# Feature-major projections of a two-layer decoder: one 512-column matmul over the tokens' high and low parts, a second of 256 columns, and four PSUM banks a chunk

## The chip, the cores and the metric

The kernel runs on one core of a Trainium2 chip. Its times are device microseconds: the median of three runs, and one profiled execution from which all rows below come. In the rows PE is the matrix engine (TensorE) and PEld its loading of weights, DVE the vector engine (VectorE), ACT the scalar engine (ScalarE), POOL GpSimd, SP the engine that issues most transfers. PSUM is the memory in which matmuls add up their results; the kernel uses it in banks of 128 x 512 fp32 numbers.

## The reference

256 tokens of width 2048 pass through two layers, each x = x + mixer(rms_norm(x)), and one last norm. The first mixer is a gated linear recurrence (HGRN2), the second a sparse attention with a compressed, a selected and a windowed branch. Both begin with one wide projection and end with an output projection; everything is fp32.

```python
def hgrn2_mixer(h, w_in, lb, head_gain, w_out):
    proj = (h @ w_in).reshape(B, S, 4, HGRN_HEADS, HGRN_HEAD_DIM)
    q, f_pre, v, z = proj[:, :, 0], proj[:, :, 1], proj[:, :, 2], proj[:, :, 3]
    ...
    o = rms_norm(o, head_gain) * jax.nn.silu(z)
    return o.reshape(B, S, HGRN_WIDTH) @ w_out

def nsa_mixer(h, w_in, ...):
    proj = h @ w_in
    q, k_c, v_c, k_s, v_s, k_w, v_w, gate_logits, z = jnp.split(proj, split_at, axis=-1)
    ...
    o = jnp.einsum('bshc,bshcd->bshd', gates, out).reshape(B, S, NSA_WIDTH) * jax.nn.silu(z)
    return o @ w_out
```

## The kernel before, in words

**Precision by parts.** Each fp32 operand of a large product is split into a high part (rounded, of type `fp32r`) and a low part, the rest (`fp32r` as well). A product of a and b is then three matmuls added up in PSUM: high a with high b, high a with low b, low a with high b. `mm3` (L148 to L150) issues them; so nearly all matmuls of the kernel have line L150. The tokens stand transposed in `xh` and `xl`, 16 tiles of 128 features by 256 tokens each.

**Pieces.** All weight matrices are walked in one list, `plan`. An entry is a piece: 128 rows by 1024 columns of weights, loaded by one 512 KB transfer on SP's queue into one of 6 `raw` buffers. For a chunk of 512 output features a piece holds two of the 16 k-tiles. ScalarE casts a piece to its high part (`emit_hi`, L132) and VectorE subtracts to get the low part (`emit_lo`, L142), both some four pieces ahead of TensorE (`SPLIT_AHEAD`), into buffers that come free when TensorE has done with an older piece. So ScalarE's casts and VectorE's subtractions run at TensorE's pace, and while they wait they hold up what is queued behind them.

**Chunks.** A chunk of kind "t" is feature-major: the weights are loaded as the stationary operand, 128 x 128 at a time, and the 256 tokens move past, so that one output tile is 128 features by 256 tokens. There are 20 such chunks of four tiles each: f and hq of four groups in the first layer (forget gate and query), then kc, vc, ks, kw, and q0 to q3 and z0 to z3 in the second. Two tiles share a PSUM bank; a chunk takes two of the pool's four banks (`main_bank`, names `mainps`) and the next chunk the other two. In a piece the k-tile is the outer loop and the tile f the inner one (`feature_major`, L170). 20 chunks x 16 k-tiles x 4 tiles make 1280 groups of three matmuls. A chunk of kind "n" is token-major: the tokens are stationary and 512 columns of weights move.

**What sets the order.** Nothing is reordered afterwards: each engine runs its instructions as the program issues them. `flush` (L249) walks the plan: first what the last chunk left to do (`finished`, the chunk's `done`), then one step of every running generator (`advance`), then the casts and loads that have come due (`prefetch`), then the piece's matmuls, then one more step of every generator. The work after a chunk (scaling by the row norms, the recurrence, the attention of a head) is written as generators whose `yield`s space it over the pieces. So a chunk's results are read from PSUM one iteration after its last matmul, behind that iteration's work. A second pool of four banks (`auxps`) holds scores, logits and transposes.

**The second layer's attention.** For each head, logits go through a biased copy with a maximum on VectorE (L868), exponentials on ScalarE (L875), a division by the sum (L884 and L886), and seven transposes on TensorE (L895 to L898). Buffers named `zs` (two of 128 x 512) hold a chunk's scaled result: kz, ks, qs or zs by turns; for z chunks they end with `yl` (L992), the low part of the gated output.

Of the kernel before, what the change touches and what calls it, by code (L numbers as in the profile page):

```python
# [45 lines left out]
def kernel(ctx: ExitStack, tc: tile.TileContext, x, norm_gains, final_gain, rel_bias,  # L46
# [56 lines left out]
    def add_chunk(w, c0, ncols, kind, src, done=None, before=None, late=False, extra=None, cuts=None):  # L103
        n = max(1, PIECE // ncols)
        if cuts is None:
            cuts = [list(range(k, min(k + n, KT))) for k in range(0, KT, n)]
        ch = dict(w=w, c0=c0, n=ncols, kind=kind, src=src, done=done, before=before, late=late)
        for i, kts in enumerate(cuts):
            plan.append((ch, kts, i == len(cuts) - 1))
            for more in (extra or {}).get(i, ()):  # L110
                more()
# [40 lines left out]
    def emit_products(i, between=None):  # L152
# [6 lines left out]
        if kts[0] == 0:  # L159
            if ch["kind"] == "t":  # L160
                ch["ps"] = [main_bank() for _ in range(n // 256)]
# [8 lines left out]
        def feature_major(k, hv, lv):  # L170
            for f in range(n // P):
                fs = slice(f * P, (f + 1) * P)
                mm3(ch["ps"][f // 2][:, (f % 2) * S:(f % 2 + 1) * S], hv[:, fs], lv[:, fs],
                    ah[:, k, :], al[:, k, :], k == 0 and f % 2 == 0, k == KT - 1)
# [8 lines left out]
        if ch["late"] and kts[0] * n >= PIECE:  # L183
# [6 lines left out]
            return  # L190
        for j, k in enumerate(kts):
            if ch["kind"] == "t":
                feature_major(k, hv[:, j], lv[:, j])
            else:
                token_major(k, hv[:, j], lv[:, j], (0, 1))
            if j == 0 and between:
                between()
# [51 lines left out]
    def flush():  # L249
        start_piece(2)  # L250
        finished = None
        for i, (ch, kts, last) in enumerate(plan):
# [10 lines left out]
            emit_products(i, (lambda: start_piece(i + 3)) if starting else None)  # L263
            if last and ch["done"]:
# [8 lines left out]
    xh = xgp.tile([P, KT, S], F32R, name="xh")  # L273
    xl = xgp.tile([P, KT, S], F32R, name="xl")
# [16 lines left out]
    hgain = pcol[:, 0, 48:49]  # L291

# [116 lines left out]
    def f_of(s, ps):  # L409
        for a in range(2):  # L410
            HG["F", a] = HG["pool"].tile([P, 512], F32, tag=f"Fg{a}", name="Fg")
            HG["K", a] = HG["pool"].tile([P, 512], F32, tag=f"Kg{a}", name="Kg")
            nc.vector.tensor_mul(pair(HG["K", a]), pair(ps[a]), rb2)
# [18 lines left out]
    def q_done(ps):  # L432
        for a in range(2):
            QQ = HG["pool"].tile([P, 2, 512], F32, tag=f"QQ{a}", name="QQ")
            nc.vector.tensor_mul(pair(QQ[:, 0]), pair(ps[a]), rbq2)
            HG["Q", a] = QQ

# [132 lines left out]
    for s in range(4):  # L570
        def on_f(ps, s=s):
            if s == 0:
                open_hg()
            if s == 0:
                run(bcast_rows(rbc, rbcq, rstd0))
                run(store_bias(), 8)
            run(f_of(s, ps), 1 if s == 0 else 0)

        def on_q(ps):
            q_done(ps)  # L580
# [8 lines left out]
        add_chunk(w_in1, 2048 + 512 * s, 512, "t", X, on_f, before=split_x if s == 0 else None,  # L589
                  cuts=[[0], [1]] + [[k, k + 1] for k in range(2, KT, 2)] if s == 0 else None)  # L590
        add_chunk(w_in1, 512 * s, 512, "t", X, on_q)
# [96 lines left out]

    def kc_done(name, *args):
        def done(ps):  # L690
            if name == "kc":
                open_ns()
            kz = [NS["p2"].tile([P, 2, S], F32, tag="zs", name="kz") for _ in range(2)]
            for j in range(2):
                nc.vector.tensor_mul(kz[j], pair(ps[j]), rb2)
# [59 lines left out]
    def split_of(src, hi, lo, col=None):  # L755
# [6 lines left out]
        yield  # L762
        yield
# [21 lines left out]
    def k_done(off):  # L785
        def done(ps):
            ks = [NS["p2"].tile([P, 2, S], F32, tag="zs", name="ks") for _ in range(2)]
            for j in range(2):
                nc.vector.tensor_mul(ks[j], pair(ps[j]), rb2)
# [7 lines left out]
    def vw_done(j):  # L797
        n = 280 if j == 0 else 232

        def done(ps):  # L800
            gate = NS["gate"]
            run(split_of([p[:, :n] for p in ps], *([t[:, tt, 280 * j:280 * j + n] for tt in range(2)] for t in NS["Vw"]),
                         [rstd1[:, tt:tt + 1] for tt in range(2)]))
# [10 lines left out]
    def q_done1(g):  # L814
        def done(ps):
            qs = [NS["p2"].tile([P, 2, S], F32, tag="zs", name="qs") for _ in range(2)]
            for a in range(2):
                nc.vector.tensor_mul(qs[a], pair(ps[a]), rbq2)
# [144 lines left out]
    def z_done1(g):  # L963
        def done(ps):
            run(gated(g, ps, NS.pop(("o", g))))
        return done

    def gated(g, ps, ov):
        ks = [slice(4 * g + 2 * a, 4 * g + 2 * a + 2) for a in range(2)]
        zs = [NS["p2"].tile([P, 2, S], F32, tag="zs", name="zs") for _ in range(2)]  # L970
# [170 lines left out]
```

## Time and profile before

| | |
|---|---|
| median of 3 runs | 993.58 us (993.15 to 994.56) |
| profiled execution | 993.57 us |
| its span (first to last instruction) | 991.7 us |
| mean granted TensorE clock, of 1 | 0.998 |
| TensorE busy | 978.8 us |
| VectorE, ScalarE busy | 630.3 us, 519.1 us |
| moved by DMA | 179.14 MB |

The profiled execution takes 1.9 us more than its span. Busy times of TensorE overlap, since a matmul is issued while the one before it is still running: a matmul's row gives its start and its duration from issue to end, and the time that it costs TensorE is the distance to the next start. In rows of a timeline the first number is the start in us from the span's start, the second the time that the engine was busy with the row's instructions (x2 are two of a kind in a row), then engine, line, operation, the tile that is written and the tiles that are read, and their shapes. In square brackets stands the idle time ahead of it, and what ended it.

### The profile page before, as it was taken

To read this page: it belongs to the slowest core of one execution; us is meant where nothing else is said; L and a number is where in the kernel's file an instruction comes from. 1 tells how busy PE (TensorE), PEld (TensorE's weight loads), DVE (VectorE), ACT (ScalarE), POOL (GpSimd) and SP (SyncE) were. 2 spreads that over 40 slices of the span, in tenths; PEclk is the share of its full clock that TensorE was granted. 3 is DMA by queue.
4 is the path that set the end of the run, shared out by engine and by line. 5 is a ranking of instruction groups with operands and counts; after the bars stand their busy time and mean duration, and the time that the engine had idled before them with its cause. 6 is when DMAs were issued, how large, how long until landed. Compare 5 with 4: busy or idle time off the path is not lost.

```text
span 991.7 us, 19895 instructions
## 1 busy us (share of the span) xinstructions
PE 978.8 (99%) x8001; PEld 906.0 (91%) x8001; DVE 630.3 (64%) x1194; ACT 519.1 (52%) x896; POOL 51.2 (5%) x154
## 2 busy tenths in 40 slices
PE   8999999999999999999999999999999999999997
PEld 7988998889978997888899999899999999998886
DVE  6767466846683668465555655454877787775664
ACT  6634553445344533545544554444767877875442
POOL 3101000100010001010011000000000000000000
PEclk9999999999999999999999999999999999999999
DMA  9655565556556555657777776575454545456662
GB/s 319 195 150 172 167 181 147 170 167 184 157 151 191 169 152 149 210 162 244 248 220 220 210 212 187 166 226 182 128 154 139 155 128 160 139 165 230 204 216 100
DMA packets 102621, 179.14 MB, mean 181 GB/s; under 512 B 6016, under 2 KB 25056, under 8 KB 102400
## 3 DMA queue, kind: packets, MB, share of 16 engines
q1 hardware_dynamic: 100512, 171.86, 57.3%
q0 software_dynamic: 1680, 5.46, 1.7%
q8 instruction: 63, 1.03, 0.4%
q10 hardware_dynamic: 336, 0.54, 0.2%
q14 instruction: 30, 0.25, 0.1%
HBM read 173.62 MB, written 4.22 MB: 179 GB/s over the span
## 4 chain that ended last, share of the span: by engine, by line
PE 97%; ACT 1%; DMA 1%; issue 1%; DVE 0%; SPq 0%; POOLq 0%; POOL 0%; DVEq 0%
PE mainps L150 86%; PE auxps L150 5%; PE auxps L468 2%; PE auxps L895 1%; DMA xt<-in_x_dram 1%; PE auxps L479 0%; PE auxps L312 0%; PE auxps L527 0%; PE auxps L526 0%; PE auxps L525 0%; PE auxps L483 0%; PE auxps L625 0%; PE auxps L550 0%; PE auxps L897 0%; PE auxps L474 0%
## 5 line engine op out<-in xcount | busy, mean ns | idle before, releaser
L132 ACT CAST hi<-raw 128x1024 fp32r<-128x1024 f32 (+3 forms) x317 | 328.5, 1038 | 324.2 <-PE mainps L150 313.8
L142 DVE TENSOR_TENSOR lo<-raw,hi 128x1024 fp32r<-128x1024 f32 (+3 forms) x317 | 380.4, 1208 | 175.9 <-ACT hi L132 174.9
L150 PE MATMUL mainps<-xh,hi 128*128 128x256 f32 x1280 | 366.3, 286 | 0.0
L150 PE MATMUL mainps<-xl,hi 128*128 128x256 f32 x1280 | 362.8, 283 | 0.0
L150 PE MATMUL mainps<-xh,lo 128*128 128x256 f32 x1280 | 362.8, 283 | 0.0
L150 PEld LDWEIGHTS mainps<-xh,hi 128*128 128x128 f32 x1280 | 245.5, 192 | 0.8 <-ACT hi L132 0.4
L150 PEld LDWEIGHTS mainps<-xl,hi 128*128 128x128 f32 x1280 | 245.6, 192 | 0.2
L150 PEld LDWEIGHTS mainps<-xh,lo 128*128 128x128 f32 x1280 | 245.3, 192 | 0.0
L150 PE MATMUL mainps<-hi,xh 128*128 128x512 f32 (+1 forms) x352 | 134.5, 382 | 0.0
L150 PE MATMUL mainps<-lo,xh 128*128 128x512 f32 (+1 forms) x352 | 131.0, 372 | 0.0
L150 PE MATMUL mainps<-hi,xl 128*128 128x512 f32 (+1 forms) x352 | 131.0, 372 | 0.0
L150 PE MATMUL mainps<-hi,yh 128*128 128x512 f32 (+1 forms) x288 | 106.0, 368 | 0.0
L150 PE MATMUL mainps<-hi,yl 128*128 128x512 f32 (+1 forms) x288 | 105.4, 366 | 0.0
L150 PE MATMUL mainps<-lo,yh 128*128 128x512 f32 (+1 forms) x288 | 105.3, 366 | 0.0
L150 PEld LDWEIGHTS mainps<-hi,xl 128*128 128x128 f32 x352 | 66.1, 188 | 11.7
L150 PEld LDWEIGHTS mainps<-hi,xh 128*128 128x128 f32 x352 | 66.1, 188 | 11.6
L150 PEld LDWEIGHTS mainps<-lo,xh 128*128 128x128 f32 x352 | 66.2, 188 | 10.2
L150 PEld LDWEIGHTS mainps<-hi,yl 128*128 128x128 f32 x288 | 54.4, 189 | 8.8
L150 PEld LDWEIGHTS mainps<-hi,yh 128*128 128x128 f32 x288 | 54.4, 189 | 8.5
L150 PEld LDWEIGHTS mainps<-lo,yh 128*128 128x128 f32 x288 | 54.4, 189 | 8.5
L875 ACT ACTIVATE L<-L,mx 128x128 f32<-128x128 f32 (+1 forms) x96 | 37.5, 392 | 24.3 <-DVE mx L870 24.2
L913 DVE TENSOR_TENSOR pl<-auxps,ph 128x512 fp32r<-128x512 f32 (+1 forms) x32 | 17.5, 556 | 16.3 <-ACT ph L909 14.7
(241 smaller groups left out, 861.4 us busy)
## 6 DMA issues: line engine op xcount, KB each, us to landing
raw<-in_hgrn_w_in_dram SPq DMA_DIRECT2D x127, 512.0 KB, 3.7
raw<-in_nsa_w_in_dram SPq DMA_DIRECT2D x104, 512.0 KB, 3.8
raw<-in_hgrn_w_out_dram SPq DMA_DIRECT2D x32, 512.0 KB, 4.9
raw<-in_nsa_w_out_dram SPq DMA_DIRECT2D x32, 512.0 KB, 4.3
raw<-in_nsa_w_in_dram SPq DMA_DIRECT2D x10, 420.0 KB, 3.4
xt<-in_x_dram SPq DMA_DIRECT2D x8, 256.0 KB, 7.9
raw<-in_x_dram SPq DMA_DIRECT2D x4, 512.0 KB, 4.5
x_dram<-x POOLq DMA_DIRECT2D x4, 512.0 KB, 6.3
```

Source lines behind the costliest of these rows:

```text
L132: nc.scalar.copy(hi[:, :m], raw[:, :m])
L142: nc.vector.tensor_sub(lo[:, :m], raw[:, :m], hi[:, :m].bitcast(F32))
L150: nc.tensor.matmul(dst, a, b, start=first and n == 0, stop=last and n == 2, skip_group_check=True)
L468: nc.tensor.matmul(dst[32 * b:32 * b + 32, i0 % 4:(i1 - 1) % 4 + 1, j, :], Kg[:, cs], QQ[:, q0:2, cs], start=True, stop=True, tile_positio ...
L875: nc.scalar.activation(dst, dst, AF.Exp, bias=mx[:, i:i + 1], accum_out=sm[:, i:i + 1])
L895: nc.tensor.transpose(t1[:, i * P:(i + 1) * P], l[:, c0:c0 + P], ident)
L913: nc.vector.tensor_sub(pl[:, ks, hh, :], t, ph[:, ks, hh, :].bitcast(F32))
```

## The change

The tokens' two parts now lie side by side in one tile, `xx`, as 128 x 2 x 256 for each k-tile. For a weight tile, one matmul of 512 columns multiplies the high weights with both parts: the bank's first half gets high times high, the second half high times low. A second matmul of 256 columns adds low weights times high tokens into the second half. So a tile of 128 x 256 outputs takes a whole bank as two partial sums, and a chunk takes all four banks of the pool.

In a piece the tile f is now the outer loop and the two k-tiles the inner one. Behind a chunk's last matmuls and ahead of the `advance` of the same iteration stands a new call, `take`, which empties the four banks (`gather`): four copies of the second halves by ScalarE, then four additions of the first halves by VectorE, into the buffers that held the scaled result before. The `done` of the next iteration multiplies in place there. Three smaller edits go with it: the pools of the two mixers are opened in the first `take`, the value split of the window branch does its subtraction without the two steps between (`apart=0`), and the gated output's last step comes one half-piece earlier (5 to 4).

```diff
         if kts[0] == 0:
             if ch["kind"] == "t":
-                ch["ps"] = [main_bank() for _ in range(n // 256)]
+                ch["ps"] = [main_bank() for _ in range(n // P)]
...
-        def feature_major(k, hv, lv):
-            for f in range(n // P):
-                fs = slice(f * P, (f + 1) * P)
-                mm3(ch["ps"][f // 2][:, (f % 2) * S:(f % 2 + 1) * S], hv[:, fs], lv[:, fs],
-                    ah[:, k, :], al[:, k, :], k == 0 and f % 2 == 0, k == KT - 1)
+        def feature_major(f, k, hv, lv):
+            fs, ps = slice(f * P, (f + 1) * P), ch["ps"][f]
+            nc.tensor.matmul(ps, hv[:, fs], xx[:, k].rearrange("p a t -> p (a t)"), start=k == 0, stop=False,
+                             skip_group_check=True)
+            nc.tensor.matmul(ps[:, S:], lv[:, fs], xh[:, k], start=False, stop=k == KT - 1, skip_group_check=True)
...
+        if ch["kind"] == "t":
+            for f in range(n // P):
+                for j, k in enumerate(kts):
+                    feature_major(f, k, hv[:, j], lv[:, j])
+                if f == 1 and between:
+                    between()
+            return
         for j, k in enumerate(kts):
-            if ch["kind"] == "t":
-                feature_major(k, hv[:, j], lv[:, j])
-            else:
-                token_major(k, hv[:, j], lv[:, j], (0, 1))
-            if j == 0 and between:
-                between()
+            token_major(k, hv[:, j], lv[:, j], (0, 1))
...
             emit_products(i, (lambda: start_piece(i + 3)) if starting else None)
+            if last and ch.get("take"):
+                ch["take"](ch["ps"])
             if last and ch["done"]:
                 finished = lambda ch=ch: ch["done"](ch.get("ps"))
...
-    xh = xgp.tile([P, KT, S], F32R, name="xh")
-    xl = xgp.tile([P, KT, S], F32R, name="xl")
+    xx = xgp.tile([P, KT, 2, S], F32R, name="xx")
+    xh, xl = xx[:, :, 0], xx[:, :, 1]
...
+    def gather(ps, outs):
+        outs = [o[:, a * S:(a + 1) * S] for o in outs for a in range(2)]
+        for p, o in zip(ps, outs):
+            nc.scalar.copy(o, p[:, S:])
+        for p, o in zip(ps, outs):
+            nc.vector.tensor_add(o, p[:, :S], o)
...
-    def f_of(s, ps):
+    def f_take(ps):
+        if "pool" not in HG:
+            open_hg()
         for a in range(2):
             HG["F", a] = HG["pool"].tile([P, 512], F32, tag=f"Fg{a}", name="Fg")
             HG["K", a] = HG["pool"].tile([P, 512], F32, tag=f"Kg{a}", name="Kg")
-            nc.vector.tensor_mul(pair(HG["K", a]), pair(ps[a]), rb2)
+        gather(ps, [HG["K", a] for a in range(2)])
+
+    def f_of(s):
+        for a in range(2):
+            nc.vector.tensor_mul(pair(HG["K", a]), pair(HG["K", a]), rb2)
...
+    def zs_take(ps):
+        if "p2" not in NS:
+            open_ns()
+        NS["zs"] = [NS["p2"].tile([P, 2, S], F32, tag="zs", name="zs") for _ in range(2)]
+        gather(ps, [flat(z) for z in NS["zs"]])
...
-    def split_of(src, hi, lo, col=None):
+    def split_of(src, hi, lo, col=None, apart=2):
...
-        yield
-        yield
+        for _ in range(apart):
+            yield
...
-                         [rstd1[:, tt:tt + 1] for tt in range(2)]))
+                         [rstd1[:, tt:tt + 1] for tt in range(2)], apart=0))
...
-            qs = [NS["p2"].tile([P, 2, S], F32, tag="zs", name="qs") for _ in range(2)]
+            qs = NS["zs"]
             for a in range(2):
-                nc.vector.tensor_mul(qs[a], pair(ps[a]), rbq2)
+                nc.vector.tensor_mul(qs[a], qs[a], rbq2)
...
-    def gated(g, ps, ov):
+    def gated(g, zs, ov):
...
-        steps_between = (3, 2, 5) if g + 1 < G else (1, 2, 2)
+        steps_between = (3, 2, 4) if g + 1 < G else (1, 2, 2)
```

How this moves instructions is shown at two places of the second layer, where the attention's work meets the end of a rewritten chunk. On TensorE, the end of q1 and the start of q2 in the kernel before (`mainps` are the chunk's banks, the transposes of the head's probabilities `L` go to `auxps`):

```order
L150 MATMUL mainps<-xh,hi 128x256
L150 MATMUL mainps<-xl,hi 128x256
L150 MATMUL mainps<-xh,lo 128x256
L895 MATMUL auxps<-ident,L 128x128 x4
L897 MATMUL auxps<-ident,L 128x128 x2
L898 MATMUL auxps<-ident,L 47x128
L150 MATMUL mainps<-xh,hi 128x256
L150 MATMUL mainps<-xl,hi 128x256
L150 MATMUL mainps<-xh,lo 128x256
```

The same place in the changed kernel:

```order
L173 MATMUL mainps<-xx,hi 128x512
L175 MATMUL mainps<-xx,lo 128x256
L920 MATMUL auxps<-ident,L 128x128 x4
L922 MATMUL auxps<-ident,L 128x128 x2
L923 MATMUL auxps<-ident,L 47x128
L173 MATMUL mainps<-xx,hi 128x512
L175 MATMUL mainps<-xx,lo 128x256
```

Three products have become two, the seven transposes stand where they stood, and the first product behind them writes a bank that the chunk before has filled.

On VectorE, the end of q3, where `yl` of z0 and the attention's copies (`pl`, `qs`) stand. Before:

```order
L886 TENSOR_SCALAR L<-L,sm 128x15
L142 TENSOR_TENSOR lo<-raw,hi 128x1024
L992 TENSOR_TENSOR yl<-zs,yh 128x512 x2
L818 TENSOR_TENSOR qs<-mainps,rbcq 128x512 x2
L913 TENSOR_TENSOR pl<-auxps,ph 128x4x128
L913 TENSOR_TENSOR pl<-auxps,ph 128x2x128
```

And in the changed kernel:

```order
L911 TENSOR_SCALAR L<-L,sm 128x15
L1016 TENSOR_TENSOR yl<-zs,yh 128x512 x2
L142 TENSOR_TENSOR lo<-raw,hi 128x1024
L303 TENSOR_TENSOR zs<-mainps,zs 128x256 x4
L843 TENSOR_TENSOR zs<-zs,rbcq 128x512 x2
L938 TENSOR_TENSOR pl<-auxps,ph 128x4x128
L938 TENSOR_TENSOR pl<-auxps,ph 128x2x128
```

`yl` has moved ahead of the next piece's low part, and the four additions (L303) stand behind that low part and ahead of the multiplications. ScalarE's row at the same place, before:

```order
L884 ACTIVATE L<-L,sm 128x256 x2
L132 CAST hi<-raw 128x1024
L909 CAST ph<-auxps 128x4x128
L909 CAST ph<-auxps 128x2x128
L911 CAST pc<-auxps 15x128 x2
L132 CAST hi<-raw 128x1024
L758 CAST qh<-qs 128x512
```

And in the changed kernel:

```order
L909 ACTIVATE L<-L,sm 128x256 x2
L132 CAST hi<-raw 128x1024
L301 COPY zs<-mainps 128x256 x4
L934 CAST ph<-auxps 128x4x128
L934 CAST ph<-auxps 128x2x128
L936 CAST pc<-auxps 15x128 x2
L132 CAST hi<-raw 128x1024
L783 CAST qh<-zs 128x512
```

The four copies (L301) have come in behind a piece's cast and ahead of the casts of the transposed probabilities (`ph`, `pc`).

## Rows read from the trace of the kernel before

**Rows 1.** Page, busy time and share of each engine, number of instructions.

```profile
PE 978.8 (99%) x8001; PEld 906.0 (91%) x8001; DVE 630.3 (64%) x1194; ACT 519.1 (52%) x896; POOL 51.2 (5%) x154
```

**Rows 2.** Page, the chain of work that ended last, shares by engine.

```profile
PE 97%; ACT 1%; DMA 1%; issue 1%; DVE 0%; SPq 0%; POOLq 0%; POOL 0%; DVEq 0%
```

**Rows 3.** Groups by form: number of instructions, busy us, mean ns of one, idle before.

```profile
L150 PE MATMUL mainps<-xh,hi 128*128 128x256 f32 x1280 | 366.3, 286 | 0.0
```

**Rows 4.** Timeline of TensorE: two stretches of products, and hq0 to its next chunk.

```profile
20.19 0.28 PE L150 MATMUL mainps<-xh,lo 128*128 128x256 f32 x1
...
21.99 0.28 PE L150 MATMUL mainps<-xh,lo 128*128 128x256 f32 x1
...
59.99 0.28 PE L150 MATMUL mainps<-xh,lo 128*128 128x256 f32 x1
...
60.11 0.40 PE L150 MATMUL mainps<-hi,xh 128*128 128x512 f32 x1
...
60.34 0.40 PE L150 MATMUL mainps<-lo,xh 128*128 128x512 f32 x1
...
61.27 0.39 PE L150 MATMUL mainps<-hi,xl 128*128 128x512 f32 x1
...
62.63 0.39 PE L150 MATMUL mainps<-hi,xl 128*128 128x512 f32 x1
```

**Rows 5.** Groups by form: a cast and an addition of 128x256 from PSUM.

```profile
L909 ACT CAST ph<-auxps 128x256 fp32r<-128x256 f32 x16 | 6.1, 378 | 0.0
L1061 DVE TENSOR_TENSOR fin_x<-mainps,raw 128x256 f32<-128x256 f32 x2 | 0.8, 424 | 4.3 <-PE mainps L150 4.3
```

**Rows 6.** Timeline of ScalarE and VectorE at the end of hq0.

```profile
57.31 1.05 ACT L132 CAST hi<-raw 128x1024 fp32r<-128x1024 f32 x1 [1.83 <-PE mainps L150]
...
60.92 1.28 DVE L453 TENSOR_TENSOR QQ<-QQ,Fg 128x512 f32<-128x512 f32 x2
```

**Rows 7.** Timeline at the end of f0, all engines.

```profile
36.55 0.19 POOL L78 TENSOR_SCALAR rstd<-ssq 128x2 f32<-128x2 f32 x1 [12.55 <-DVE ssq L330]
...
36.75 0.28 PE L150 MATMUL mainps<-xh,lo 128*128 128x256 f32 x1
...
36.95 1.05 ACT L132 CAST hi<-raw 128x1024 fp32r<-128x1024 f32 x1 [1.21 <-PE mainps L150]
```

**Rows 8.** Timeline at the end of the window branch's value chunks.

```profile
661.47 0.28 PE L150 MATMUL mainps<-xh,hi 128*128 128x256 f32 x1
...
662.23 0.80 ACT L760 ACTIVATE Vwh<-mainps,rstd 128x232 fp32r<-128x232 f32 x2
```

**Rows 9.** Timeline at the end of q1.

```profile
710.15 1.03 ACT L132 CAST hi<-raw 128x1024 fp32r<-128x1024 f32 x1
...
710.54 0.60 PE L895 MATMUL auxps<-ident,L 128*128 128x128 f32 x4
...
711.22 0.36 PE L150 MATMUL mainps<-xh,hi 128*128 128x256 f32 x1
```

**Rows 10.** Timeline at the end of q3.

```profile
803.51 1.22 DVE L142 TENSOR_TENSOR lo<-raw,hi 128x1024 fp32r<-128x1024 f32 x1
...
804.06 0.60 PE L895 MATMUL auxps<-ident,L 128*128 128x128 f32 x4
...
804.65 1.29 DVE L992 TENSOR_TENSOR yl<-zs,yh 128x512 fp32r<-128x512 f32 x2
```

**Rows 11.** Timeline at the end of z0, and the next head's first division and transposes.

```profile
773.61 1.23 DVE L142 TENSOR_TENSOR lo<-raw,hi 128x1024 fp32r<-128x1024 f32 x1
...
773.84 0.29 PE L150 MATMUL auxps<-Kh,qh 128*128 128x272 f32 x1
...
774.95 0.27 PE L150 MATMUL mainps<-xh,hi 128*128 128x256 f32 x1
...
779.46 0.29 DVE L886 TENSOR_SCALAR L<-L,sm 128x128 f32<-128x128 f32 x1
...
780.69 0.60 PE L895 MATMUL auxps<-ident,L 128*128 128x128 f32 x4
```

## What was predicted, before the changed kernel had run

> **What bounds the kernel now.** I read the page first. Its busy table gives TensorE 99% of a span of 991.7 us [rows 1], and the chain that ended last is 97% TensorE [rows 2]. So the time is the sum of TensorE's start-to-start spacings, and another engine counts only where TensorE waits for it. The groups by form then give the part that the change rewrites: three products per weight tile, each 128x256, 1280 of each [rows 3]. Their busy times overlap (286 ns is issue to end), so I went to the timeline for the spacings [rows 4]. From 20.19 to 21.99 lie 15 gaps of 256 columns: 0.120 us each. From 61.27 to 62.63 lie 6 gaps of 512 columns: 0.227 us each. The difference, 0.107 us for 256 columns, is streaming at the full clock; what is left, 0.013 us, is paid once per matmul at either width. Last I read ScalarE, VectorE and TensorE at the ends of the rewritten chunks, because there the change adds a wait.
>
> **The change, part by part.** Below, T is the moment at which a rewritten chunk's last product gives TensorE free; f0 to f3 and hq0 to hq3 are the forget and query chunks of the first layer, q0 to q3 and z0 to z3 those of the second.
>
> Products. Removed: 3 x 1280 matmuls of 256 columns, 3 x 0.120 = 0.360 us per weight tile. Added: one of 512 and one of 256, 0.227 + 0.120 = 0.347. The columns are the same 768, and one fixed part of 0.013 us goes. 1280 x 0.013 = 16.6 us. The new mixed order stands once in the trace, where a query chunk meets the next one: 256 at 59.99, 512 at 60.11, the next at 60.34, so 0.12 and 0.23 also beside the other width [rows 4]. The bounds of the pair: nothing gained (0.360), and 0.227 + 0.108 = 0.335 if the short one fell to the spacing of the short transposes (seven start within 0.68 us, 710.54 to 711.22, and the last is a narrow one, so 0.108 for a full one is the low end) [rows 9]. That is 0 to 32 us; I take 16.6, the value of the row with both widths.
>
> The Trainium skill speaks against this gain: "TensorE: Matmul & The Clock Gate", section "Back-to-back issue gap", puts the spacing at N/2.4 plus a fixed 2.5 ns. By it the merge is worth 1280 x 2.5 ns = 3.2 us, less than the waits below, and the kernel would get slower. The trace does not agree: its spacings leave 13 ns at both widths, and I go by the rows.
>
> Emptying. A chunk now has two partial sums in each of four banks, all four that the pool has. Added per chunk: four ScalarE copies of 128x256 from PSUM, 0.378 each by the cast of that shape, and four VectorE additions, 0.424 each by the addition of that shape with one side in PSUM [rows 5]. That is 20 x 1.51 = 30 us of ScalarE and 20 x 1.70 = 34 us of VectorE. The later multiplications keep their number and shape and only change their source, behind the emptying: counted at nothing. Both engines are idle a third of the span or more [rows 1], so this costs only where the next chunk's first product finds its bank full. Bank f is complete (3-f) x 0.694 us before T, since two k-tiles of one f now run together, and is wanted again f x 0.694 after T.
>
> Calm ends, 15 of 20. Ahead of the copies ScalarE has the cast for three pieces later. It ends at 58.36 for a T of 60.11 [rows 6], so 1.75 before T, after bank 0 is complete. Copy and addition then end 0.9 us before T. The last bank: a cast that waited for the last product began 0.20 after that product's start (36.75, 36.95), so 0.08 after T [rows 7]; copy and addition end at T + 0.9, and the bank is wanted at T + 2.1. No wait, with 1.2 us to spare. If that cover is gone (a copy that waits for the whole chunk) it is rival three.
>
> Scores after hq0 to hq3. VectorE's multiplications now start after the additions. In the old run they ended at 62.20, T + 2.1 [rows 6], and the score matmuls stand behind one piece of twelve 512-column products, near T + 2.8. Now: additions to T + 0.9, then four passes of 0.6 (two took 1.28) to T + 3.3, while TensorE needs the first half at T + 2.8 and the second, half a microsecond of score matmuls later, at T + 3.4. I charge 0.1 each, 0.4 us.
>
> f0 to hq0. The first copy writes memory that GpSimd's first step of the norm still reads. That step ended at 36.74 for a T of 36.87 [rows 7]; it hangs on ScalarE's paced casts, so it moves forward nearly as T does (0.7 against 0.8). Copy and addition after it: T + 0.9. TensorE wants the bank at T: 0.9 us.
>
> Window values to q0. q0's third bank was read last by the value split. Its two ScalarE reads run from 662.23 to 663.03, with T = 661.47 [rows 8]; the first ends half way, near T + 1.2, VectorE's subtraction for it, now right behind, costs about an addition (0.42) and a few hundredths of handing over and ends near T + 1.8. The bank is wanted at T + 1.4: 0.4 us.
>
> q1 to q2. Here the attention's bursts delay ScalarE: the cast ahead of the copies ends at 711.18, T + 0.64 [rows 9], and 0.84 after a T that comes 0.2 earlier (two shorter pieces since the logits that set the burst off). Copy to 1.13, addition to 1.6. TensorE has seven transposes in between, 0.7 us. Wait 0.9 us.
>
> q3 to z1. The same, but two subtractions for yl, 0.65 us apart at 804.65, stood behind the low-part subtraction of 803.51 to 804.73 [rows 10]; now they stand ahead of it, and the copies reuse the zs buffers that they read. Low part to T + 0.67 + 0.2 + 1.2 = T + 2.1, first addition T + 2.5, with T = 804.06, less 0.7: 1.8 us.
>
> z0 to q3, and z2 to z3, which repeats it. VectorE's low part ends at 774.84, T + 1.0, now T + 1.1 [rows 11]; the first addition T + 1.5, and TensorE has 1.1 us of logits first (773.84 to 774.95): 0.4. The next head's bias pass then starts 1.3 later. Its first divided weights stood 0.94 us before the transposes (779.75, 780.69). That slack is used up by 1.3 + 0.1 of delay and 0.2 of shorter pieces, less the 0.4 already waited: about 0.5 with the later transposes. Together 0.9, twice 1.8 us.
>
> Sum: -16.6 + 0.4 + 0.9 + 0.4 + 0.9 + 1.8 + 1.8 = -10.4 us. The profiled execution took 993.57 (991.7 of it span); the median of the runs is 993.58, so the same base. Forecast 983.2 us.
>
> **Rivals.** 1. No waits: the bursts move with TensorE and the banks are always free. For it: the calm ends have 1.2 us to spare. Against: both helpers are late at the ends shown [rows 9 to 11]. 993.6 - 16.6 = 977.
>
> 2. The helpers lag through the attention. Eight of the twenty ends lie there, ScalarE and VectorE get 12 and 14 us more in that stage, and a late addition delays the next head's bias pass, exponentials and transposes. If each of the eight ends costs 1.5 to 2 us the waits are 14 us: 991. Against: ScalarE still waits for TensorE 1.83 and 1.21 us before a cast in the calm rows [rows 6, 7], so a lag has room to drain there; how much room the attention leaves no row here shows.
>
> 3. The banks come free only as a whole: copies start after T, not one by one. Then each of 20 ends waits for 0.08 + 0.378 + 0.424, some 0.9 us, and with the attention's extra 3 us the price is 21 us: 993.6 - 16.6 + 21 = 998, slower. It decides from 0.83 us per end on (16.6 / 20). Against: in the built order each copy has a wait of its own, and f is now the outer loop.
>
> 4. The pair does not give its fixed part back: what is paid once per matmul belongs to the change of weights and hides under neither width, so 2.5 ns of the 13 go: 993.6 - 3.2 + 6.2 = 996.6, slower. Against: the mixed neighbours [rows 4]. The Trainium skill's spacing rule, named above, would have this result.
>
> **How the numbers follow.** My forecast with waits of 2 to 10 us: 65%, 979 to 987. Rival 1: 8%. Rival 2: 14%, 987 to 993. Rival 3: 5%, rival 4: 5%; the rest, 3%, is anything that I have not seen, on the slow side. The range that leaves out no more than 2 in 10 is 978 to 991. A difference under 0.2%, 2 us, is what a measurement of this kernel cannot tell from none. Faster by more than that (under 991.6) is the forecast, rival 1 and most of rival 2: 0.85; within it 0.06; slower 0.09.
>
> **What would show it.** The groups of TensorE should have 1280 of 128x512 and 1280 of 128x256 in the place of 3840, with starts 0.227 and 0.120 apart; the granted clock stays at 1.00. TensorE should be seen waiting for the additions at the ends of f0, q1, q3, z0 and z2, near 1 us, and nowhere else. A spacing of 0.357 for the pair is rival 4; a wait near 0.9 at every one of the 20 ends is rival 3; waits of 2 us and more at q0 to z3, or long waits of transposes for L911 and L909, are rival 2. I am wrong if the time is over 991 or the gain over 16 us.

## The result, and the profile after

| | before | after |
|---|---|---|
| median | 993.75 us (993.15 to 994.56) | 988.27 us (987.06 to 989.39) |
| ratio of after to before | | 0.9946, 95% interval 0.9934 to 0.9958 |
| profiled execution, its span | 993.57, 991.7 us | 988.16, 986.3 us |

The kernel became faster by 5.4 us, between 4.2 and 6.6 by the interval. The forecast was 983.2 us with a range of 978 to 991. Its sign was right and the time lies within the range, but the gain that it forecast, 10.4 us, is about twice the one that came.

The busy table and the chain's shares by engine, for the changed kernel; they answer to [rows 1, 2]:

```profile
PE 968.3 (98%) x6721; PEld 836.3 (85%) x6721; DVE 658.1 (67%) x1274; ACT 543.7 (55%) x976; POOL 52.4 (5%) x154
PE 92%; ACT 3%; DVE 2%; issue 1%; DMA 1%; SPq 0%; POOL 0%; DVEq 0%; POOLq 0%; ACTq 0%
```

1280 matmuls are gone (8001 to 6721), VectorE is busy 28 us more and ScalarE 25 us more, and 5% of the chain now lies on these two, where it was 1%. The groups by form show the pairs in the place of [rows 3], with 4.1 us of idle time ahead of the long ones, nearly all ended by the emptying's additions:

```profile
L173 PE MATMUL mainps<-xx,hi 128*128 128x512 f32 x1280 | 455.3, 398 | 4.1 <-DVE zs L303 3.2 <-DVE Kg L303 0.7 <-DVE Vwl L793 0.2
L175 PE MATMUL mainps<-xx,lo 128*128 128x256 f32 x1280 | 357.6, 279 | 0.0
```

All waits of TensorE in the changed kernel (line, who ended it, total us, times, longest):

```profile
PE auxps L1125 <- DMA gn<-in_norm_gains_dram: 3.6, 1, 3.6
PE mainps L173 <- DVE zs L303: 3.2, 4, 1.7
PE auxps L326 <- DMA xt<-in_x_dram: 1.8, 1, 1.8
PE auxps L920 <- DVE L L911: 1.0, 1, 1.0
PE mainps L173 <- DVE Kg L303: 0.7, 1, 0.7
PE mainps L173 <- DVE Vwl L793: 0.2, 1, 0.2
```

And all waits of TensorE in the kernel before:

```profile
PE auxps L1101 <- DMA gn<-in_norm_gains_dram: 3.8, 1, 3.8
PE auxps L312 <- DMA xt<-in_x_dram: 0.9, 1, 0.9
PE auxps L895 <- DVE L L886: 0.6, 1, 0.6
```

In the changed kernel L303 stands for five waits, four (zs) after q1, q3, z0 and z2 and one (Kg) after f0, and Vwl for the start of q0. These are the places that the prediction named. Behind the other fifteen of the twenty ends no product waits.

**Where the time went.** Three stretches, each between two starts of products: up to the first product of hq0, from there to the last product of z3, and the rest. First the two rows of the kernel before, then those of the changed one:

```profile
36.87 0.28 PE L150 MATMUL mainps<-xh,hi 128*128 128x256 f32 x1
895.77 0.28 PE L150 MATMUL mainps<-xh,lo 128*128 128x256 f32 x1
```

```profile
38.39 0.50 PE L173 MATMUL mainps<-xx,hi 128*128 128x512 f32 x1 [0.68 <-DVE Kg L303]
...
890.28 0.28 PE L175 MATMUL mainps<-xx,lo 128*128 128x256 f32 x1
```

The middle stretch shrank from 858.90 to 851.89 us, by 7.0. The first grew by 1.5, and the last is the same to 0.1 us (95.94 and 96.03). So 7 us were won in 19 chunks and 1.5 lost ahead of them. Of the 1.5, 0.84 is the new wait at the end of f0; the rest is there before f0 begins, whose first product starts at 9.81 us and not at 9.12, since the first tokens arrived later.

In the middle stretch I took the distance from a weight tile's first product to the next tile's, for tiles with nothing between them, the few per cent of stray long ones left out (about as many before as after). Its mean over the 19 chunks fell from 359.6 to 348.7 ns: 1216 x 10.9 ns = 13.3 us. The waits that TensorE has now and had not before are, by what each spacing has over its usual value: q0 0.37, q1 1.14, q3 1.96, z0 0.45, z2 0.46, scores 4 x 0.16, two late transposes 0.22 each, and an old wait of transposes in z2 that grew from 0.75 to 1.15. Together 5.9 us. 13.3 - 5.9 = 7.4, and 7.0 were measured.

### The profile page after: what moved, and what is told of

It reads as the page before. It is cut to its first block, busy times and chain, and to the rows that moved or that the text cites. A ratio compares the mean times of both kernels' runs of the same rounds, so it can differ in the third digit from the quotient of the medians.

```text
span 986.3 us, 17479 instructions
## 1 busy us (share of the span) xinstructions
PE 968.3 (98%) x6721; PEld 836.3 (85%) x6721; DVE 658.1 (67%) x1274; ACT 543.7 (55%) x976; POOL 52.4 (5%) x154
## 4 chain that ended last, share of the span: by engine, by line
PE 92%; ACT 3%; DVE 2%; issue 1%; DMA 1%; SPq 0%; POOL 0%; DVEq 0%; POOLq 0%; ACTq 0%
PE mainps L150 40%; PE mainps L173 28%; PE mainps L175 14%; PE auxps L150 4%; PE auxps L491 2%; ACT L L900 1%; DVE lo L142 1%; DMA xt<-in_x_dram 1%; ACT hi L132 1%; PE auxps L920 1%; PE auxps L326 0%; PE auxps L502 0%; PE auxps L549 0%; PE auxps L550 0%; PE auxps L506 0%
## 5 line engine op out<-in xcount | busy, mean ns | idle before, releaser
L173 PE MATMUL mainps<-xx,hi 128*128 128x512 f32 x1280 | 455.3, 398 | 4.1 <-DVE zs L303 3.2
L175 PE MATMUL mainps<-xx,lo 128*128 128x256 f32 x1280 | 357.6, 279 | 0.0
L173 PEld LDWEIGHTS mainps<-xx,hi 128*128 128x128 f32 x1280 | 240.8, 188 | 59.1 <-DVE zs L303 4.1
L175 PEld LDWEIGHTS mainps<-xx,lo 128*128 128x128 f32 x1280 | 241.8, 189 | 0.2
L150 PE MATMUL mainps<-hi,xx 128*128 128x512 f32 (+1 forms) x704 | 211.8, 377 | 0.0
L150 PEld LDWEIGHTS mainps<-hi,xx 128*128 128x128 f32 x704 | 128.4, 188 | 23.2
L150 PE MATMUL mainps<-lo,xx 128*128 128x512 f32 (+1 forms) x352 | 130.8, 372 | 0.0
L150 PEld LDWEIGHTS mainps<-lo,xx 128*128 128x128 f32 x352 | 66.1, 188 | 10.1
L303 DVE TENSOR_TENSOR zs<-mainps,zs 128x256 f32<-128x256 f32 x48 | 18.7, 420 | 13.2 <-ACT zs L301 12.2
L893 DVE CUSTOM_DVE_ANT_0 L<-auxps,bias 128x128 f32<-128x128 f32 (+1 forms) x96 | 22.0, 291 | 3.4 <-PE auxps L150 2.7
```

What stands on the lines that cost most here:

```text
L150: nc.tensor.matmul(dst, a, b, start=first and n == 0, stop=last and n == 2, skip_group_check=True)
L173: nc.tensor.matmul(ps, hv[:, fs], xx[:, k].rearrange("p a t -> p (a t)"), start=k == 0, stop=False, skip_group_check=True)
L175: nc.tensor.matmul(ps[:, S:], lv[:, fs], xh[:, k], start=False, stop=k == KT - 1, skip_group_check=True)
L303: nc.vector.tensor_add(o, p[:, :S], o)
L893: nc.vector.tensor_tensor_reduce(out=dst, in0=lg, in1=b, op0=ALU.add, op1=ALU.max, scale=1.0, scalar=-3e38, accum_out=mx[:, i:i + 1])
```

## The experiments

The ratios are to the kernel before on the same chip, and they are what to compare: 0.9946 and 0.9951 for the changed kernel in two sets of runs. 1 us is 0.001.

### The 512-column product cut in two again

```diff
-            nc.tensor.matmul(ps, hv[:, fs], xx[:, k].rearrange("p a t -> p (a t)"), start=k == 0, stop=False, ...)
+            nc.tensor.matmul(ps[:, :S], hv[:, fs], xh[:, k], start=k == 0, stop=False, ...)
+            nc.tensor.matmul(ps[:, S:], hv[:, fs], xl[:, k], start=False, stop=False, ...)
```

> The changed kernel with its 512-column product cut in two of 256 columns again; the four banks a chunk, the tile as outer loop and the emptying stay. Theory (the whole gain is the fixed part of one matmul less, 10.8 ns per weight tile by the two traces, 359.5 against 348.7 in undisturbed tiles): 1280 x 10.8 ns come back, 13.8 us, and the waits at the chunk ends stay, so about 1002 us, slower than the kernel before by the price of the emptying, some 7 to 8 us. Rival (the pair gives nothing back, and the gain comes from the new order or from the emptying behind the products): within 2 us of the changed kernel, 988.

998.75 us, ratio 1.0063 (1.0051 to 1.0075): slower than the kernel before by 6 us, and than the changed one by 11 to 12. TensorE's waits are shorter than with the pair; that each chunk takes longer and so leaves the helpers more time would explain it, and is argued:

```profile
PE mainps L173 <- DVE zs L303: 2.4, 4, 1.3
...
PE mainps L173 <- DVE Kg L303: 0.6, 1, 0.6
```

The tile's distance is 359.6 ns again, chunk for chunk that of the kernel before to within 0.4 ns. So the merge is what gains, and order, banks and emptying together cost some 6 us. The theory held; its 1002 was 2 to 3 us high, and 1.2 of that by the lists of waits are the waits, which it left at their length.

### The k-tile as outer loop

```diff
-            for f in range(n // P):
-                for j, k in enumerate(kts):
+            for j, k in enumerate(kts):
+                for f in range(n // P):
                     feature_major(f, k, hv[:, j], lv[:, j])
```

> The changed kernel with the k-tile as outer loop of a piece again and the tile f as the inner one. Then bank f is complete only (3-f) x 0.347 us before the end T of the chunk, and wanted f x 0.347 after it. Theory (a bank is copied 0.3 us after the one before it and added 0.36 us after the one before it, so that the banks come free as fast as they are wanted, and only the first bank's delay behind the helpers' queues counts): no new waits at the calm ends, the same waits as before at f0, q1, q3, z0 and z2: 988 to 990 us. Rival (the order with the tile outside is what makes the emptying cheap): 0.4 to 0.9 us more at each of 20 ends, 996 to 1006 us.

990.7 us, ratio 0.9976 (0.9968 to 0.9985): 3 us slower than the changed kernel. The ends of the first layer still have no wait after hq0 to hq3. Where it differs in the waits is q0, where the value split's banks are now wanted earlier; the group was 0.2 in the changed kernel:

```profile
PE mainps L173 <- DVE zs L303: 3.3, 4, 1.8
...
PE mainps L173 <- DVE Vwl L793: 0.9, 1, 0.9
```

The rival's 996 to 1006 is out: the order with the tile outside is not what makes the emptying cheap. In the profiled execution the stretch from hq0 to z3 took 857.2 us, 5.3 more than in the changed kernel, and began 2.1 earlier. Of the 5.3 us, 0.7 is the wait at q0 and 1216 x 1.2 ns = 1.5 are products: the mean distance rose to 349.8 ns, with 353 in hq1 and hq2, which had 346.7. Another 1.5 us are five pairs in z1 whose long products took 0.43 us each and whose short ones 0.21, nearly twice their usual. There the granted clock is 0.50, the lower of its two levels (1.2 GHz), from 802.2 to 805.7 us. TensorE had sat idle 1.84 us for q3's additions just before; but in the changed kernel it waited 1.72 us at that place and kept the full clock, so what lowered it here is open, as are the remaining 1.6 us.

### Two long, two short

The part "h" issues the 512-column product, "l" the one of 256.

```diff
-                for j, k in enumerate(kts):
-                    feature_major(f, k, hv[:, j], lv[:, j])
+                for part in "hl":
+                    for j, k in enumerate(kts):
+                        feature_major(f, k, hv[:, j], lv[:, j], part)
```

> The changed kernel with the four matmuls of one tile in a piece in the order 512, 512, 256, 256 columns and not 512, 256, 512, 256. In the busy chunks (ks, q2 to z1) the spacings of a pair repeat over three tiles as 241+120, 236+113, 233+117, on average 353, and 347 in the calm ones. Theory (the strict alternation of long and short lets the spacings fall into the slower of two rhythms): with two of a kind in a row the slow rhythm goes, 347 everywhere, 1280 x 1.7 ns = 2.2 us less, 986 us. Rival (what slows the pair in the busy chunks comes from outside TensorE): 988 us, unchanged.

986.78 us, ratio 0.9945 (0.9932 to 0.9958): no change. The distances did change: 348.2 to 348.5 from hq0 to q1 and up to 350.3 behind it, where the changed kernel has 346.7 to 352.0. The slower rhythm is gone, and the faster one with it; the means are equal, 348.6 to 348.7 in both. In ks, where the pairs now take 348.3 for 351.5, the order of widths matters, and a steady load from outside TensorE can't be the whole reason. Behind q1 the spacings still rise, which leaves room for one. As an edit it is worth nothing.

### Cast and subtraction behind the emptying

```diff
+            behind = ch is not None and last and ch.get("take") and not starting
-            if not starting:
+            if not starting and not behind:
                 prefetch(i, SPLIT_AHEAD)
...
             if last and ch.get("take"):
                 ch["take"](ch["ps"])
+            if behind:
+                prefetch(i, SPLIT_AHEAD)
```

> The changed kernel with one move: in the last piece of a rewritten chunk, the cast to the high part and the subtraction to the low part of a piece needed three pieces later are issued behind the emptying, not ahead of the products. Theory (the waits at q1, q3, z0 and z2 are nothing but these two instructions ahead of the copies and additions in their engines' order): the wait of 1.1 us at q1 falls to about 0.1, that of 2.0 at q3 to 0.6 (its copies wait for the buffers that yl reads), those of 0.45 at z0 and z2 go, and the late transposes of 0.2 behind them; f0 stays at 0.8. Together 3.6 us, 984.7 us. Rival (the helpers have no slack in the attention stage, and what is put behind is late later): the waits come back at the next products as waits for the low part, 988 us or more.

994.85 us, ratio 1.0017 (1.0008 to 1.0026): 7 us slower than the changed kernel, and 10 off my theory. The aim was met, and the price came elsewhere. TensorE's waits:

```profile
PE auxps L494 <- DVE QQ L479: 4.4, 4, 1.1
...
PE auxps L923 <- DVE L L914: 2.3, 4, 1.3
...
PE auxps L150 <- ACT hi L132: 1.4, 2, 0.7
PE mainps L173 <- DVE zs L306: 0.9, 2, 0.7
```

The waits for the additions fell from 3.2 to 0.9 us (by the spacings 0.45 are left at q1 and 0.90 at q3, where 0.1 and 0.6 were expected). The new ones: 4.4 for the first layer's scores, 1.3 more for the transposes, 1.4 for a cast. VectorE's rows after hq0 show why:

```profile
60.43 1.22 DVE L142 TENSOR_TENSOR lo<-raw,hi 128x1024 fp32r<-128x1024 f32 x1
61.56 1.28 DVE L462 TENSOR_TENSOR QQ<-QQ,rbcq 128x512 f32<-128x512 f32 x2
...
62.76 1.28 DVE L479 TENSOR_TENSOR QQ<-QQ,Fg 128x512 f32<-128x512 f32 x2
```

The low part now stands between the additions and the multiplications, for whose result the score matmuls wait: they start 1.1 us late, four times. I had asked what the moved instructions were ahead of, and not what they would be put ahead of. The rival was right about the time, and not about the place: the largest new waits are in the first layer, and none of them is for the low part itself.

### The changed kernel once more

> The changed kernel itself once more, beside the others of this set. In its first profile TensorE's first chunk ended 1.3 us later than the sum allows, since the first tokens arrived late (a wait of 1.8 us for them, 0.9 in the kernel before). Theory (that is chance of the run): a ratio between 0.993 and 0.995 to the kernel before again, and in its profile the first chunk's last product somewhere between 35.5 and 37.5 us. Rival (the change makes the start later): that product at 37.5 us again.

988.27 us, ratio 0.9951 (0.9939 to 0.9964). f0's last product began at 37.43 us again, so the theory of chance got no support here. But something else came out. TensorE's rows from the same place of hq0, in the first execution of the changed kernel and in this one:

```profile
44.26 0.39 PE L173 MATMUL mainps<-xx,hi 128*128 128x512 f32 x1
44.49 0.27 PE L175 MATMUL mainps<-xx,lo 128*128 128x256 f32 x1
44.61 0.40 PE L173 MATMUL mainps<-xx,hi 128*128 128x512 f32 x1
...
45.99 0.40 PE L173 MATMUL mainps<-xx,hi 128*128 128x512 f32 x1
```

```profile
44.35 0.40 PE L173 MATMUL mainps<-xx,hi 128*128 128x512 f32 x1
44.59 0.28 PE L175 MATMUL mainps<-xx,lo 128*128 128x256 f32 x1
44.70 0.40 PE L173 MATMUL mainps<-xx,hi 128*128 128x512 f32 x1
...
46.12 0.40 PE L173 MATMUL mainps<-xx,hi 128*128 128x512 f32 x1
```

Five tiles take 1.73 us in the one and 1.77 in the other, 346 and 354 ns each, and so over the whole of hq0: 346.7 and 353.4. The same program at the same place runs in either rhythm.

### Without the additions

```diff
         for p, o in zip(ps, outs):
             nc.scalar.copy(o, p[:, S:])
-        for p, o in zip(ps, outs):
-            nc.vector.tensor_add(o, p[:, :S], o)
```

> The changed kernel without the four additions of the emptying: a chunk's result is the second halves alone, the high times high sums are left out. ScalarE's copies free the banks by themselves, and VectorE loses 34 us of work. Theory (the waits are the chain of cast, copy and addition at each end): at q1 the wait falls from 1.1 to 0.6 us, at q3 from 2.0 to 0.8, at f0 from 0.8 to 0.3; those of z0 and z2 (0.45 each), the transposes behind them (0.2 each) and the scores' four times 0.16 go. Together 4.1 us, 984 us. Rival (the waits hang on ScalarE's queue alone): less than 1 us gained, 987 to 988 us.

982.55 us, ratio 0.9902 (0.9887 to 0.9917): 4.9 us less than the changed kernel by the two ratios. TensorE's waits at the ends:

```profile
PE mainps L173 <- ACT zs L301: 0.8, 2, 0.4
...
PE mainps L173 <- ACT Kg L301: 0.2, 1, 0.2
```

By the spacings, q1 fell to 0.69 us (0.6 expected), q3 to 0.60 (0.8), f0 to 0.39 (0.3), and the waits of z0, z2, the two transposes and the scores are gone. From hq0 to z3 it takes 847.22 us, 4.7 under 851.89. So the additions' part of the waits is shown, and what is left at q1, q3 and f0 ends with ScalarE's copies: the chain of cast, copy and addition. This kernel leaves out a part of the result; it only prices the additions.

### Eight long, eight short

```diff
-            for f in range(n // P):
-                for part in "hl":
+            for part in "hl":
+                for f in range(n // P):
                     for j, k in enumerate(kts):
                         feature_major(f, k, hv[:, j], lv[:, j], part)
```

(against the kernel with two long and two short)

> The changed kernel with all eight 512-column products of a piece first and its eight of 256 columns behind them. Undisturbed spacings of one width are 227 and 120, 347.2 for a pair. Theory (the rhythm belongs to the order of widths: 346.7 or 353 when they alternate one by one, 348.3 two by two): 347.2 to 347.5 in every chunk, 1280 x 1.5 ns = 2 us less; against that the banks are complete only 0.24 us apart, so the first addition ends 0.2 us after T, and some 12 calm ends wait 0.2 us each: about 988 us again. Rival (the busy chunks are slowed from outside TensorE): spacings of 350 and more there.

994.66 us, ratio 1.0015 (1.0006 to 1.0024): 6.5 us slower than the changed kernel, where I expected none. Both terms were too small. Calm ends wait 0.37 us each and not 0.2, since the copy waits for the product's end, 0.28 us after its start, which I had not counted. At the end of hq0 the first bank's last product is the second of the eight short ones, begun at 61.35 and ended at 61.63:

```profile
61.23 1.11 PE L177 MATMUL mainps<-xx,lo 128*128 128x256 f32 x8
...
61.67 1.20 ACT L304 COPY QQ<-mainps 128x256 f32<-128x256 f32 x4 [1.98 <-PE mainps L177]
62.07 0.76 DVE L306 TENSOR_TENSOR QQ<-mainps,QQ 128x256 f32<-128x256 f32 x2 [3.92 <-ACT QQ L304]
...
62.55 0.50 PE L150 MATMUL mainps<-hi,xx 128*128 128x512 f32 x1 [0.21 <-DVE QQ L306]
```

And a row of eight long products does not run at 227: in f1 its spacings go 229, 234, 235, 225, 230, 236, 229, on average 231. With 119 for the short ones that is 350 a pair, not 347. My theory, that a run of one width takes the spacing of the token-major chunks, is refuted for a row of eight; in hq1 the first five take 228 to 236, and only the last three 226 or 227.

### Two edits at the waits

```diff
-    ssqp = sp.tile([P, 2, 4], F32, name="ssqp")
-    ssq = sp.tile([P, 2], F32, name="ssq")
+    ssqp = const.tile([P, 2, 4], F32, name="ssqp")
+    ssq = const.tile([P, 2], F32, name="ssq")
...
-        steps_between = (3, 2, 4) if g + 1 < G else (1, 2, 2)
+        steps_between = (3, 2, 3) if g + 1 < G else (1, 2, 2)
```

> The changed kernel with two edits. The sums of squares of the first norm lie in a pool of their own, so that f0's copies don't reuse memory that GpSimd still reads. The gated output's low part is issued one half-step earlier (3 for 4), into 1.46 us in which VectorE waits idle for the exponentials. Theory: f0's wait of 0.8 us goes, and q3's falls from 2.0 to 1.2, what ScalarE's cast ahead of the copies sets at q1 too: 1.6 us less than the changed kernel. Rival (something else is late in their place: another reader of that memory, or the division behind the low part): unchanged within 0.3 us.

986.63 us, ratio 0.9940 (0.9928 to 0.9952). f0's wait is gone and q3's fell to 1.37 us; of the group zs 2.7 us are left:

```profile
PE mainps L173 <- DVE zs L303: 2.7, 4, 1.1
```

1.6 us were expected and 1.1 came (0.9951 to 0.9940), but the intervals of the two ratios overlap. The theory holds by the rows; by the times alone it is not shown. The mean distance rose from 349.1 to 349.6, as the slower rhythm ruled in kc and q0 this time.

### The kernel before once more, and a last version

> The kernel before, once more, for the start alone. In its first profile the first chunk's last product began at 36.75 us, in the two of the changed kernel at 37.43, though each of the chunk's 64 weight tiles is shorter there. Theory (when the first tokens arrive is chance of the execution): that product somewhere else between 35.5 and 38 us. Rival (the kernel before starts earlier as a rule): 36.75 again within 0.1 us.

In this one execution f0's last product began at 37.27 us (36.75 before). In the kernels that begin like the changed one it lies between 35.32 and 38.19. So the start differs by some 3 us from kernel to kernel and by 0.5 in two executions of one; of the 1.5 us by which the first stretch grew, the 0.7 ahead of f0's first product may be of this kind. From its first product to its last f0 took 27.63 us in the first execution of the kernel before, 28.05 in this one, and 27.62 and 27.67 in the two of the changed kernel.

The last version is the two edits with two long, two short:

> The changed kernel with the edits that paid or cost nothing together: f0's sums in a pool of their own, the gated output's low part one half-step earlier, and the products of a tile in the order 512, 512, 256, 256. Theory (waits and rhythm add up: 1.4 us of waits go, and 348.3 in nearly every chunk stands for a mixture of 347 and 353): 1.5 to 2.5 us under the changed kernel, a ratio of 0.993 to the kernel before. Rival (the order of the pair only trades one rhythm for another): the same as with the two edits alone, 0.994.

986.55 us, ratio 0.9934 (0.9920 to 0.9947). It has the lowest ratio of those that compute the whole result, 1.2 to 1.7 us under the changed kernel, again with overlapping intervals; its mean distance is 348.6. It beats the kernel before clearly. That it beats the changed kernel the rows of f0 and q3 suggest, and the times alone do not show it; nor do they exclude the rival's 0.994.

## Why the prediction was right, and what was off

**The bound and the mechanism** were right. The time is the sum of TensorE's starts, a fixed part per matmul is paid at either width, and merging two products saves one. Cutting the pair again gave back 11 to 12 us, and the old distance. So rival 4's time is refuted. Whether the 13 ns belong to the matmul or to its weight load is not decided: every matmul has a load of its own in both kernels (8001 and 6721 of each in the busy tables), and the merge took away one of each. The Trainium skill's formula, N/2.4 + 2.5 ns in "TensorE: Matmul & The Clock Gate", section "Back-to-back issue gap", would make the merge worth 3.2 us, as an estimate. Between hq0 and z3 it was 13.3 by the rows. The Trainium skill calls this formula the gap of an isolated matmul and says there that in a real kernel weight loads and matmuls both set the spacing, which the prediction left out.

**The step that was mis-sized** is the first term: "1280 x 0.013 = 16.6 us". It measured 13.3 us, for two reasons that the runs show. In 19 chunks the distance fell by 10.9 ns, not 13. The calm ones did give 13.3 (360.0 to 346.7 in hq1 to hq3), as the row of mixed neighbours said; but one crossing of widths, at [rows 4], stood for 1280, and strict alternation has a second rhythm of 352 to 353 ns, in which long products take 241, 236 and 233 ns by turns. It appeared in ks and q2 to z1. Even in the calm chunks the pair's sum was right and its split was not: in hq1 the long product took 232 ns and the short one 115, for 227 and 120.

And f0, for which the term counted 0.8 us, gave nothing. Its products took 0.40 us less, but the transposes of the tokens among them 0.38 us more. TensorE begins f0 at half pace in both kernels (256 columns 213 ns apart, later 120). That ended at 11.6 us in the kernel before and at 12.8 in the changed one, where the trace's record of the granted clock begins, at 1.00. The second four transposes stand behind that moment in the one and ahead of it in the other; so they took 0.36 and 0.71 us to the next product. First the kernel before, then the changed one:

```profile
8.35 1.12 PE L312 MATMUL auxps<-ident,xt 128*128 128x128 f32 x4 [0.94 <-DMA xt<-in_x_dram]
...
9.12 0.56 PE L150 MATMUL mainps<-xh,hi 128*128 128x256 f32 x1
...
11.74 0.60 PE L312 MATMUL auxps<-ident,xt 128*128 128x128 f32 x4
```

```profile
9.05 1.12 PE L326 MATMUL auxps<-ident,xt 128*128 128x128 f32 x4 [1.84 <-DMA xt<-in_x_dram]
9.81 0.78 PE L173 MATMUL mainps<-xx,hi 128*128 128x512 f32 x1
...
11.24 1.06 PE L326 MATMUL auxps<-ident,xt 128*128 128x128 f32 x4
```

The wait for the tokens ends ahead of f0's first product, so it delays f0 and does not stretch it. In the kernel before's second execution the same spacing of 213 ns stands beside a recorded clock of 0.50 (1.2 GHz) from 10.1 to 13.5 us, after TensorE had waited 1.83 us for the tokens until 8.80; there the transposes fell into the slow part too, and f0 took 28.05 us. So 0.4 us of f0's gain shows against that execution and none against the first. That the half pace of the other two is this lower clock is concluded from the equal spacing.

**The waits** were right in their places and near in size. Forecast and measured, in us: f0 0.9 and 0.84; q0 0.4 and 0.37; q1 0.9 and 1.14; q3 1.8 and 1.96; scores 0.4 and 0.64; z0 and z2 1.8 and 1.35, to which the transposes in z2 add 0.40 that I had not named. Sum 6.2 and 6.7.

Four of these sums do not quite follow from their own terms. At q0, 1.2 and 0.42 and the handing over end near T + 1.7 and not 1.8, which makes 0.3; 0.4 lay closer to the 0.37 measured, by luck. At q1 the copy ends at T + 1.22 by its own 0.378 and not at 1.13, and the wait stays 0.9. At q3 the two subtractions for yl take 1.3 by [rows 10] and not 1.2, which makes 1.9. Behind z0 and z2, delay, shorter pieces and slack leave 0.3 for the transposes and not 0.5; 0.22 came.

The rows at q1 show the chain as it was worked out, ScalarE's cast late behind the burst, then copy, addition, product:

```profile
703.02 1.03 ACT L132 CAST hi<-raw 128x1024 fp32r<-128x1024 f32 x1
...
703.78 0.27 PE L923 MATMUL auxps<-ident,L 128*47 128x128 f32 x1
...
704.07 1.20 ACT L301 COPY zs<-mainps 128x256 f32<-128x256 f32 x4
...
704.48 0.76 DVE L303 TENSOR_TENSOR zs<-mainps,zs 128x256 f32<-128x256 f32 x2 [0.45 <-ACT zs L301]
...
704.96 0.50 PE L173 MATMUL mainps<-xx,hi 128*128 128x512 f32 x1 [0.90 <-DVE zs L303]
```

At q3 the same chain stands behind VectorE's low part, which follows yl; it answers to [rows 10]:

```profile
797.15 1.28 DVE L1016 TENSOR_TENSOR yl<-zs,yh 128x512 fp32r<-128x512 f32 x2
...
798.35 1.21 DVE L142 TENSOR_TENSOR lo<-raw,hi 128x1024 fp32r<-128x1024 f32 x1
...
799.49 0.74 DVE L303 TENSOR_TENSOR zs<-mainps,zs 128x256 f32<-128x256 f32 x2
...
799.96 0.50 PE L173 MATMUL mainps<-xx,hi 128*128 128x512 f32 x1 [1.72 <-DVE zs L303]
```

The copies took 0.37 to 0.38 us and the additions 0.42 each, as [rows 5] had it.

**The rivals.** Rival 1 (977) had too few waits, rival 2 (991) too many in the attention. Rival 3 did not come, as fifteen ends show; and the run with the k-tile outside shows that it is enough for the banks to be complete 0.35 us apart, and not 0.69. With eight long and eight short they are 0.24 apart, and the calm ends do wait.

**The whole sum.** The start, counted at nothing, added 0.7 us before f0's first product. 13.3 - 6.7 - 0.7 = 5.9 us, and the span shrank by 5.4. All three misses, 3.3 us of products, 0.5 of waits and 0.7 of start, went the same way. The time, 988.3, lies outside the 979 to 987 that the prediction gave to its own mechanism and in the 987 to 993 of rival 2, whose lagging helpers did not come. So the range held because it took in a rival that was wrong, and that is luck.

**What stays open**: what sets the rhythm of the pairs (the order of widths changes it, and one program had both at one place in two executions; whether something outside TensorE, at another moment in each execution, tips it from one to the other no run shows), whether the fixed part is the matmul's or its weight load's, and how much of the later start belongs to the change.

## What to carry to other kernels

Where TensorE's starts make the time, count matmuls as well as columns: the fixed part per matmul, each with a weight load of its own, was 11 to 13 ns here, and merging two products that share weights gave it back in 19 of 20 chunks. Size it by many spacings in several stages, and not by one crossing. What the merge needs, banks that are emptied before the next chunk, is priced end by end from the helpers' queues, and moving an instruction out of one wait's way asks first whose way it is put into.

## What was not expected of the hardware

Alternating matmuls of 512 and 256 columns run in one of two rhythms, 347 or 353 ns a pair, and the same program had 346.7 and 353.4 in the same chunk of two executions. Two long and two short gave 348.3, eight and eight about 350, though long products in the token-major chunks are 227 apart. In one execution the granted clock fell to 0.50 for 3.4 us in the middle of the kernel, which cost 1.5 us.
